# A two-layer trunk on one core: layer B's projection weights are split earlier and pass DRAM

## The chip, the core and the metric

The kernel runs on one core of a Trainium2 chip. The engines of the core are TensorE (PE), VectorE (DVE), ScalarE (ACT), GpSimd (POOL) and SyncE (SP), which issues most transfers. The metric is the device time in microseconds, the median of several runs. The kernel before takes 1478.44 us (three runs, 1476.97 to 1478.71).

## The reference

A sequence of 1024 rows of width 1024 passes two layers, both with an adaptive norm in front and a gated residual behind. Layer A is a gated delta rule over 8 heads of width 128. After it a shared pair of keys and values is computed once; layer B attends to it with 16 heads of width 64 and "stick-breaking" weights in place of a softmax:

```python
kv = hk @ w_kv                                      # keys and values, once
proj = h @ w_in_b                                   # layer B: queries and a gate
q = rms(proj[..., :W]);  z = proj[..., W:]
logits = q @ k.T * Dh ** -0.5
after = sum(log_keep) - cumsum(log_keep)            # log_keep = log_sigmoid(-logits), masked
o = exp(log_sigmoid(logits) + after) @ v
y = (o * silu(z)) @ w_out
```

All inputs and the output are 32-bit floats. `w_in_b` is 1024 x 2048: 1024 columns of queries, 1024 of the gate.

## The kernel before

Every product that needs full precision is done in three matmuls over operands that are split into a high and a low part: high is the operand rounded to the matmul's own 32-bit format, low is what is left (`mm3`, L110 to L113: high x high, high x low, low x high). A weight tile is loaded into `wraw` (`load_w`, L198 to L201), copied on ACT into `whi` (L194) and subtracted on DVE into `wlo` (L195). The pool `wp` holds two buffers of each.

The kernel has these stages, in order: layer A's projections and delta rule; layer A's out projection; the shared keys and values, which take up from about 690 us; layer B; and the final out projection.

Keys and values (`keys_values`, L837 to L853): eight column groups `n` of `w_kv`, 256 columns each. The first four are keys, the last four are values (the values' half). For every `n` there are two halves of the rows, and in each four steps; a step is 24 matmuls of 256 columns into one of two PSUM banks (`pj`), which ACT evacuates to `kv` (L797). Keys get a norm and are transposed; values are only stored to `v_dram` (L808, L809). After each `n`, `mod_b` prepares one eighth of layer B's input `hT`: ACT modulates it, DVE casts the high part (L834), POOL subtracts the low part (L835).

Layer B works on 8 pairs of heads. A pair has a query projection (`stage_q`, L942) and a gate projection (`stage_z`, L957). Each begins by loading and splitting one weight tile of 1024 x 128, 512 KB, so there are 16 such tiles; in order of use they are q0, z0, q1, z1 and so on. One projection is two halves of the rows with 24 matmuls of 512 columns each. Behind a half of the queries ACT makes `sqq` and the two `Qs` (L951 to L953) and DVE their low parts (L954, L955); behind a half of the gate there is `szb` (L963, L964). The attention of a pair runs between: logits on PE (L976, L977), a sigmoid on ACT (L978, `kp`), a scan on DVE (L982), transposes on PE (L997, `ptw`), the split of the weights into `wh` on ACT (L1002) and `wl` on DVE (L1004), the product with the values on PE (L1022, L1023, `pa`), and its collection in `o` (L1032, L1033).

What sets the order: PE's order is written by hand from a list of positions in time, so that steps of a projection lie between attention steps of another pair (L1098 to L1151). The order on ACT, DVE, POOL and in the DMA queues is laid by a scheduler when the kernel is built; on the chip every engine then works strictly in that order. SP issues one transfer after the other, and one that has to wait for a buffer holds those behind it.

Of the kernel before, what the change touches and what calls it, by code (L numbers as in the profile page):

```python
# [8 lines left out]
F32 = mybir.dt.float32  # L9
F32R = mybir.dt.float32r  # L10
I32 = mybir.dt.int32
AF = mybir.ActivationFunctionType
ALU = mybir.AluOpType
# [9 lines left out]
def kernel(  # L23
# [24 lines left out]
    V, S, G, PE = nc.vector, nc.scalar, nc.gpsimd, nc.tensor  # L48
    dma = nc.sync.dma_start

    P = 128
    T = x.shape[1]
    D = x.shape[2]
    NT = T // P
    ND = D // P
    HA = 8
    NC = T // P
    NPB = 8
# [8 lines left out]
    wp = ctx.enter_context(tc.tile_pool(name="wp", bufs=2, side="left"))  # L67
    dr = ctx.enter_context(tc.tile_pool(name="dr", bufs=1, space=DRAM))
# [54 lines left out]
    kTd = dr.tile([2, NPB, P, T], F32, name="kT_dram")  # L123

    vd = dr.tile([NPB, P + 1, NT, 2 * HD], F32, name="v_dram")
    gTd = dr.tile([HA * NC, P], F32, name="gT_dram")
    gate_d = dr.tile([2, D], F32, name="gate_dram")

# [61 lines left out]
    def split_w(raw, shape, pool=None, eng=None, copy=None):  # L190

        hi = (pool or wp).tile(shape, F32R, name="whi", tag="whi")
        lo = (pool or wp).tile(shape, F32R, name="wlo", tag="wlo")
        (copy or S.copy)(out=hi, in_=raw)  # L194
        (eng or G).tensor_tensor(out=lo, in0=raw, in1=hi, op=ALU.subtract)  # L195
        return hi, lo

    def load_w(src):  # L198
        raw = wp.tile([P, src.shape[0] // P, src.shape[1]], F32, name="wraw", tag="wraw")
        dma(out=raw, in_=src.rearrange("(k p) n -> p k n", p=P))  # L200
        return raw  # L201
# [151 lines left out]
    with tc.tile_pool(name="gt", bufs=1, side="right", reuse_waits="tile") as gt:  # L353
        hi, lo = w_first[0]
# [5 lines left out]
        for cc in range(NC):  # L360
# [8 lines left out]
                        op=ALU.add)  # L369
# [287 lines left out]
    for h in range(HA):  # L657
# [23 lines left out]
        if h < len(mods):  # L681
            i, part = mods[h]
# [35 lines left out]
    kp_ = kv_stack.enter_context(tc.tile_pool(name="kvp", bufs=2, side="right", reuse_waits="tile"))  # L718

    def x4(shape, dtype, name):  # L720
        return kp_.tile(shape, dtype, name=name, tag="x4", bufs=8)
# [50 lines left out]
    def kv_weights(n):  # L772
        c0 = n * 256
        parts = []
        for k0 in (0, 4):
            raw = load_w(w_kv[k0 * P:(k0 + 4) * P, c0:c0 + 256])
            if k0 == 0:
                parts.append(split_w(raw, [P, 4, 256], None, V))
            else:
                hi, lo = x4([P, 4, 256], F32R, "kwh"), x4([P, 4, 256], F32R, "kwl")  # L780
                S.copy(out=hi, in_=raw)
                V.tensor_tensor(out=lo, in0=raw, in1=hi, op=ALU.subtract)
                parts.append((hi, lo))
        return parts
# [42 lines left out]
    def mod_b(n):  # L827

        xh = x4([P, T], F32, "xhl")
        dma(out=xh, in_=xhT[n])  # L830
        S.activation(out=xh, in_=xh, func=AF.Identity, scale=mod_gs[1][:, n:n + 1], bias=mod_sh[1][:, n:n + 1])
        for hf in range(TH):
            xs = xh[:, hf * 512:hf * 512 + 512]
            V.tensor_copy(out=hT[hf][:, 0, n], in_=xs)  # L834
            G.tensor_tensor(out=hT[hf][:, 1, n], in0=xs, in1=hT[hf][:, 0, n], op=ALU.subtract)  # L835

    def keys_values():  # L837
        parts, tail = kv_weights(0), None
        yield
        for n in range(8):  # L840
            for hf in range(TH):
                if hf == 1 and n < 7:
                    nxt = kv_weights(n + 1)
                g = kv_half(n, parts, hf)
                for i in range(4):
                    next(g)
                    if i == 2 and tail:
                        next(tail, None)
                    yield
                tail = g  # L850
            parts = nxt
            mod_b(n)
        next(tail, None)  # L853

    with tc.manual_schedule(engines={PE.engine}):
        ra, kv = [rest_of_a(t) for t in range(NT)], keys_values()
        for step in "01203w142k53k64k75kk6k7k":
            next(kv if step in "wk" else ra[int(step)], None)
        for _ in kv:
            pass  # L860
# [54 lines left out]
    def project_steps(hi, lo, hf):  # L915
        ps = pj_pool.tile([P, 512], F32, name="pj", tag="pj")
        for k in range(ND):
            mm3(ps, hi[:, k], lo[:, k], hT[hf][:, 0, k], hT[hf][:, 1, k], k == 0, k == ND - 1)
            if k == 5 and sqs:
                norms(*next(iter(sqs)))  # L920
            if k < ND - 1:
                yield
        return ps
# [3 lines left out]
    def norms(p, hf):  # L927
# [7 lines left out]
        if hf == 0:  # L935
# [3 lines left out]
        V.tensor_scalar(out=nrq[p].rearrange("p t e -> p (t e)"), in0=rn, scalar1=-HD ** -0.5, scalar2=None,  # L939
                        op0=ALU.mult)  # L940

    def stage_q(p):  # L942

        q0, q1 = Qs[p, 0], Qs[p, 1] = [bp.tile([P, T], F32R, name="Qs", tag="Qs", bufs=4) for _ in range(2)]
        hi, lo = split_w(load_w(w_in_b[0][:, p * P:(p + 1) * P]), [P, ND, P], None, V)
        n2[p] = bp.tile([P, 16], F32, name="n2q", tag="n2q", bufs=2)
        for hf in range(TH):
            ps = yield from project_steps(hi, lo, hf)
            ts_ = slice(hf * 512, hf * 512 + 512)
            sqs[p, hf] = sq = bp.tile([P, 512], F32, name="sqq", tag="sqq", bufs=1)  # L950
            S.activation(out=sq, in_=ps, func=AF.Square)  # L951
            S.copy(out=q0[lo_, ts_], in_=ps[lo_])
            S.copy(out=q1[up_, ts_], in_=ps[up_])  # L953
            V.tensor_tensor(out=q0[up_, ts_], in0=ps[lo_], in1=q0[lo_, ts_], op=ALU.subtract)  # L954
            V.tensor_tensor(out=q1[lo_, ts_], in0=ps[up_], in1=q1[up_, ts_], op=ALU.subtract)  # L955
            yield
    def stage_z(p):  # L957

        hi, lo = split_w(load_w(w_in_b[0][:, D + p * P:D + (p + 1) * P]), [P, ND, P], None, V)
        for hf in (1, 0):  # L960
            ps = yield from project_steps(hi, lo, hf)
            sz[p, hf] = s = bp.tile([P, 512], F32, name="szb", tag="szb", bufs=3)
            S.activation(out=s, in_=ps, func=AF.Sigmoid)  # L963
            V.tensor_tensor(out=s, in0=ps, in1=s, op=ALU.mult)  # L964
            yield

    def weigh(p, e, t):

        n = (t + 1) * P
        d = slice(t * P, (t + 1) * P)  # L970
        q, kh, kl = Qs[p, e], Kh[p, e], Kl[p, e]
        kps[p, e, t] = kp = bp.tile([P, T], F32, name="kp", tag="kp", bufs=KPB)
        for s0 in range(0, n, 512):
            sw = min(512, n - s0)
            pl = lg_pool.tile([P, 512], F32, name="pl", tag="lg")
            PE.matmul(pl[:, :sw], q[:, d], kh[:, s0:s0 + sw], start=True, stop=False)  # L976
            PE.matmul(pl[:, :sw], q[:, d], kl[:, s0:s0 + sw], start=False, stop=True)  # L977
            S.activation(out=kp[:, s0:s0 + sw], in_=pl[:, :sw], func=AF.Sigmoid, scale=nrq[p][:, t, e:e + 1])  # L978
            if s0 + sw < n:
                yield  # L980
        kr = kp[:, :n][:, ::-1]
        V.tensor_tensor_scan(out=kr, data0=kr, data1=stick[:, T - n:][:, ::-1], initial=1.0, op0=ALU.mult,  # L982
                             op1=ALU.max)
        weighed.add((p, e, t))
        yield
# [54 lines left out]
    def projections():  # L1040
        for p in range(NPB):
            if p > 0:
                yield from stage_z(p - 1)
            yield from stage_q(p)
        yield from stage_z(NPB - 1)
# [78 lines left out]
    for i, (p, e, t) in enumerate(tiles):  # L1124
        w = weigh(p, e, t)
# [10 lines left out]
    n = 32 * NPB - 22  # L1136
# [45 lines left out]
```

## Time and profile before

| | |
|---|---|
| median of three runs | 1478.44 us |
| the profiled execution | 1474.96 us |
| its span | 1473.2 us |
| PE busy | 1378.9 us (94% of the span) |
| DVE busy | 1047.4 us (71%) |
| ACT busy | 743.7 us (50%) |
| POOL busy | 105.5 us (7%) |
| DMA | 181.15 MB, mean 123 GB/s |

One execution was profiled, and its rows are in microseconds from the start of the span. A row of the profile names a line of the kernel (L111), an engine, an operation and the tiles that it writes and reads (`out<-in`). "Idle" is the time that an engine sat without work before an instruction, with what released it. The matmuls of PE are pipelined, so their durations overlap: one of 512 columns adds about 0.23 us to the chain though it is shown with 0.4.

### The profile page before, as it was taken

The page shows a single profiled execution, that of the slowest core. Times are in us where ns is not written, and L with a number is a line of the kernel's source. Part 1 is how long each engine was busy: PE and PEld are TensorE (multiplying, and loading weights), DVE is VectorE, ACT ScalarE, POOL GpSimd, SP SyncE. Part 2 cuts the span into 40 slices and gives each one's busy share as a digit, 9 for nine tenths or more (in the row PEclk, how much of TensorE's full clock was granted, in tenths as well). Part 3 has the DMA queues.
Part 4 walks back from the last instruction along what each step waited for, and adds up shares of the span by engine and source line. Part 5 has one row for each costly group of instructions (what it writes and reads, how often), then busy time and mean ns, then how long its engine had stood idle before and what let it go on. Part 6 is the DMA issues. An engine that isn't in the chain of part 4 may idle for free.

```text
span 1473.2 us, 23359 instructions
## 1 busy us (share of the span) xinstructions
PE 1378.9 (94%) x8611; PEld 1151.5 (78%) x8611; DVE 1047.4 (71%) x2465; ACT 743.7 (50%) x1494; POOL 105.5 (7%) x105
## 2 busy tenths in 40 slices
PE   3789999999979999999799999999999999998998
PEld 0468888787867887878589999878888888885676
DVE  3768796969778787954786611388888888889332
ACT  5366645555554655431774522366666666665110
POOL 1300000000000000000220101311011011000000
PEclk9999999999989999999999999999999999999999
DMA  9244214454444353454854443624234233233511
GB/s 327 63 120 141 70 50 115 116 142 105 129 108 140 90 165 102 134 156 150 288 180 158 144 144 101 194 72 107 59 93 115 69 99 92 68 97 124 178 56 58
DMA packets 168132, 181.15 MB, mean 123 GB/s; under 512 B 36617, under 2 KB 121426, under 8 KB 168018
## 3 DMA queue, kind: packets, MB, share of 16 engines
q1 hardware_dynamic: 165586, 171.27, 38.9%
q0 software_dynamic: 2432, 8.39, 1.6%
q8 instruction: 68, 1.11, 0.3%
q14 instruction: 46, 0.38, 0.1%
HBM read 140.22 MB, written 39.40 MB: 122 GB/s over the span
## 4 chain that ended last, share of the span: by engine, by line
PE 62%; DVE 24%; ACT 6%; DMA 4%; issue 3%; SPq 0%; POOL 0%; DVEq 0%; ACTq 0%; POOLq 0%
PE pj L111 15%; PE pj L113 15%; PE pj L112 14%; DVE kp L982 8%; DVE wl L1004 2%; PE pgr L484 2%; PE ptw L997 2%; DMA mraw<-in_w_ada_dram 2%; DVE macc L150 2%; PE pa L1022 1%; PE pa L1023 1%; PE pc L174 1%; PE pl L976 1%; ACT kp L978 1%; PE pl L977 1%
## 5 line engine op out<-in xcount | busy, mean ns | idle before, releaser
L111 PE MATMUL pj<-hT,whi 128*128 128x512 f32 (+1 forms) x528 | 215.3, 408 | 6.4 <-ACT vT L421 3.5
L113 PE MATMUL pj<-hT,wlo 128*128 128x512 f32 (+1 forms) x528 | 214.5, 407 | 4.6 <-DVE wlo L195 4.4
L112 PE MATMUL pj<-hT,whi 128*128 128x512 f32 (+1 forms) x528 | 214.3, 406 | 1.3 <-POOL hT L309 1.3
L982 DVE TENSOR_TENSOR_SCAN kp<-kp,stick 128x896 f32<-128x896 f32 (+7 forms) x128 | 179.4, 1403 | 2.4 <-ACT kp L978 1.5
L978 ACT ACTIVATE kp<-pl,nrq 128x512 f32<-128x512 f32 (+1 forms) x192 | 107.0, 581 | 44.8 <-PE pl L977 36.6
L1002 ACT ACTIVATE wh<-ptw 128x512 fp32r<-128x512 f32 (+3 forms) x152 | 84.6, 557 | 74.3 <-PE ptw L997 72.6
L111 PEld LDWEIGHTS pj<-hT,whi 128*128 128x128 f32 (+1 forms) x528 | 98.4, 186 | 25.5 <-ACT vT L421 4.2
L113 PEld LDWEIGHTS pj<-hT,wlo 128*128 128x128 f32 (+1 forms) x528 | 98.4, 187 | 23.4 <-DVE wlo L195 5.8
L112 PEld LDWEIGHTS pj<-hT,whi 128*128 128x128 f32 (+1 forms) x528 | 98.3, 186 | 19.7 <-POOL hT L309 2.3
L111 PE MATMUL pj<-hbT,whi 128*128 128x512 f32 x256 | 107.4, 419 | 0.0
L195 DVE TENSOR_TENSOR wlo<-wraw,whi 128x1024 fp32r<-128x1024 f32 x55 | 67.3, 1223 | 56.3 <-ACT whi L194 49.8
L111 PE MATMUL pj<-wo,oh 128*128 128x512 f32 x256 | 103.5, 406 | 3.9 <-ACT oh L237 2.3
L113 PE MATMUL pj<-wo,ol 128*128 128x512 f32 x256 | 101.5, 397 | 0.5 <-DVE ol L238 0.5
L112 PE MATMUL pj<-wo,oh 128*128 128x512 f32 x256 | 101.8, 398 | 0.0
L113 PE MATMUL pj<-hbT,wlo 128*128 128x512 f32 x256 | 100.8, 394 | 0.0
L112 PE MATMUL pj<-hbT,whi 128*128 128x512 f32 x256 | 100.1, 391 | 0.0
L997 PE MATMUL ptw<-ident,kp 128*128 128x128 f32 x576 | 91.0, 276 | 8.1 <-DVE wl L1004 6.0
L1004 DVE SCALAR_TENSOR_TENSOR wl<-ptw,wh 128x512 fp32r<-128x512 f32 (+1 forms) x140 | 87.4, 625 | 10.3 <-ACT wh L1002 9.2
L194 ACT CAST whi<-wraw 128x1024 fp32r<-128x1024 f32 x55 | 57.8, 1051 | 67.9 <-PE pj L112 60.4
L1022 PE MATMUL pa<-wh,vt 128*128 128x256 f32 (+1 forms) x280 | 79.2, 305 | 13.0 <-DVE o L1033 11.8
L997 PEld LDWEIGHTS ptw<-ident,kp 128*128 128x128 f32 x576 | 67.8, 141 | 27.0 <-DVE wl L1004 12.7
L150 DVE SCALAR_TENSOR_TENSOR macc<-mraw,cact,macc 128x512 f32<-128x512 f32 x105 | 82.4, 785 | 5.4 <-DMA mraw<-in_w_ada_dram 4.2
(303 smaller groups left out, 3391.5 us busy)
## 6 DMA issues: line engine op xcount, KB each, us to landing
mraw<-in_w_ada_dram SPq DMA_DIRECT2D x96, 256.0 KB
wraw<-in_w_in_a_dram SPq DMA_DIRECT2D x32, 512.0 KB
mraw<-in_w_ada_kv_dram SPq DMA_DIRECT2D x32, 256.0 KB
xr<-x_dram SPq DMA_DIRECT2D x16, 512.0 KB
wraw<-in_w_kv_dram SPq DMA_DIRECT2D x16, 512.0 KB
kT_dram<-kt SPq DMA_DIRECT2D x32, 256.0 KB
wraw<-in_w_in_b_dram SPq DMA_DIRECT2D x16, 512.0 KB
Kh<-kT_dram SPq DMA_DIRECT2D x32, 256.0 KB
```

The costliest lines, as they stand in the source:

```text
L111: PE.matmul(ps, lh, rh, start=start, stop=False)
L112: PE.matmul(ps, lh, rl, start=False, stop=False)
L113: PE.matmul(ps, ll, rh, start=False, stop=stop)
L150: V.scalar_tensor_tensor(out=acc, in0=raw, scalar=cact[:, k:k + 1], in1=acc, op0=ALU.mult, op1=ALU.add)
L194: (copy or S.copy)(out=hi, in_=raw)
L195: (eng or G).tensor_tensor(out=lo, in0=raw, in1=hi, op=ALU.subtract)
L978: S.activation(out=kp[:, s0:s0 + sw], in_=pl[:, :sw], func=AF.Sigmoid, scale=nrq[p][:, t, e:e + 1])
L982: V.tensor_tensor_scan(out=kr, data0=kr, data1=stick[:, T - n:][:, ::-1], initial=1.0, op0=ALU.mult, op1=ALU.max)
L997: PE.transpose(pt[:, i], kps[p, e, 2 * g + q][:, j * P:(j + 1) * P], ident)
L1002: S.activation(out=wh[:, :nb], in_=pt[:, :nb], func=AF.Copy, bias=-1.0)
L1004: V.scalar_tensor_tensor(out=wl[:, :nb], in0=pt[:, :nb], scalar=-1.0, in1=wh[:, :nb], op0=ALU.add, op1=ALU.subtract)
L1022: PE.matmul(dst, lh, wh[:, sl], start=(j == 0), stop=False)
```

## The change

Fifteen of the sixteen weight tiles of layer B (all but q0) are split ahead of time. `presplit` is a generator of 30 steps, one for each half (512 rows) of a tile. A step loads 256 KB of raw weights on SP's queue, copies the high part on ACT, subtracts the low part in place on DVE, and stores both, 256 KB each, to the new DRAM tensor `wb_dram` from POOL's queue. Its tiles share the tag `x2k`, five buffers of 2 KB a partition, which the keys used. One step is taken after each of the 32 steps of the values' half. In layer B `weights_b` then loads the two parts, 512 KB each, straight into the buffers `whi` and `wlo`; for q0 it loads and splits as before.

```diff
+    wbd = dr.tile([2 * NPB, P, 2, ND * P], F32, name="wb_dram")
...
+    def column_of(i):
+        return i // 2 * P + (D if i % 2 else 0)
+    def presplit():
+        for i in range(1, 2 * NPB):
+            for kh in range(2):
+                src = w_in_b[0][kh * 512:kh * 512 + 512, column_of(i):column_of(i) + P]
+                raw = kp_.tile([P, 4, P], F32, name="wbr", tag="x2k", bufs=5)
+                dma(out=raw, in_=src.rearrange("(k p) n -> p k n", p=P))
+                hi = kp_.tile([P, 4, P], F32R, name="wbh", tag="x2k", bufs=5)
+                S.copy(out=hi, in_=raw)
+                lo = raw.bitcast(F32R)
+                V.tensor_tensor(out=lo, in0=raw, in1=hi, op=ALU.subtract)
+                for j, w in enumerate((hi, lo)):
+                    G.dma_start(out=wbd[i, :, j, kh * 512:kh * 512 + 512],
+                                in_=w.bitcast(F32).rearrange("p k n -> p (k n)"))
+                yield
     def keys_values():
+        pre = presplit()
...
                     if i == 2 and tail:
                         next(tail, None)
+                    if n >= 4:
+                        next(pre, None)
                     yield
...
+    def weights_b(i):
+        if i == 0:
+            return split_w(load_w(w_in_b[0][:, 0:P]), [P, ND, P], None, V)
+        parts = wp.tile([P, ND, P], F32R, name="whi", tag="whi"), wp.tile([P, ND, P], F32R, name="wlo", tag="wlo")
+        for j in range(2):
+            dma(out=parts[j].bitcast(F32).rearrange("p k n -> p (k n)"), in_=wbd[i, :, j])
+        return parts
     def stage_q(p):
-        hi, lo = split_w(load_w(w_in_b[0][:, p * P:(p + 1) * P]), [P, ND, P], None, V)
+        hi, lo = weights_b(2 * p)
...
     def stage_z(p):
-        hi, lo = split_w(load_w(w_in_b[0][:, D + p * P:D + (p + 1) * P]), [P, ND, P], None, V)
+        hi, lo = weights_b(2 * p + 1)
```

## Rows read from the trace of the kernel before

**Rows 1.** Busy time by stretch (engine us, instructions), TensorE's clock, DMA share, GB/s.

```profile
core 0: us, PE busy (x) PEld busy (x) DVE busy (x) ACT busy (x) POOL busy (x), PEclk, DMA share, GB/s
10.00:20.00 10.00, 0.00 (x0) 0.00 (x0) 3.94 (x15) 6.79 (x9) 0.00 (x0) 1.00 1.03 403
711.00:720.00 9.00, 4.58 (x24) 3.34 (x22) 6.75 (x16) 6.95 (x16) 2.66 (x4) 1.00 0.96 325
842.00:933.00 91.00, 91.00 (x770) 91.00 (x769) 15.60 (x25) 24.88 (x45) 10.64 (x10) 1.00 0.38 118
933.00:950.00 17.00, 16.98 (x84) 14.02 (x82) 5.18 (x7) 5.88 (x10) 4.67 (x7) 1.00 0.92 247
1000.00:1300.00 300.00, 288.94 (x1764) 248.31 (x1762) 261.17 (x391) 191.46 (x362) 29.81 (x21) 1.00 0.33 91
```

**Rows 2.** Waits of PE, 950 to 1310: us in total, times, longest us.

```profile
PE pa L1022 <- DVE o L1033: 6.8, 9, 1.1
PE ptw L997 <- DVE wl L1004: 5.3, 7, 1.0
```

**Rows 3.** The chain of waits around 1040: start us, us, what.

```profile
1039.18 0.24 PE pj L112
...
1039.45 1.05 ACT whi L194
1040.50 0.49 ACT sqq L951
...
1045.72 0.32 DVE o L1033
```

**Rows 4.** PE's timeline at three holes, idle before in brackets: start us, us, instruction.

```profile
992.74 0.39 PE L1022 MATMUL pa<-wh,vt 128*128 128x256 f32 x1 [1.06 <-DVE o L1033]
...
1046.10 0.39 PE L1022 MATMUL pa<-wh,vt 128*128 128x256 f32 x1 [1.05 <-DVE o L1033]
...
1258.73 0.39 PE L1022 MATMUL pa<-wh,vt 128*128 128x256 f32 x1 [1.06 <-DVE o L1033]
```

**Rows 5.** Lines of the splits: count, ns min/median/max, first and last start.

```profile
L194 ACT CAST whi<-wraw x55: 1033/1049/1120, 73.7 to 1278.7; 128x1024 fp32r<-128x1024 f32 x55
L195 DVE TENSOR_TENSOR wlo<-wraw,whi x55: 1196/1224/1260, 74.8 to 1279.8; 128x1024 fp32r<-128x1024 f32 x55
L822 ACT CAST kt<-pk x16: 567/587/653, 765.2 to 850.6; 128x512 fp32r<-128x512 f32 x16
L823 DVE TENSOR_TENSOR kt<-pk,kt x16: 679/681/692, 766.1 to 851.3; 128x512 fp32r<-128x512 f32 x16
```

**Rows 6.** Timelines of DVE and PE where layer B starts.

```profile
962.48 1.20 DVE L195 TENSOR_TENSOR wlo<-wraw,whi 128x1024 fp32r<-128x1024 f32 x1
...
966.31 0.55 PE L997 MATMUL ptw<-ident,kp 128*128 128x128 f32 x3 [0.78 <-DVE wl L1004]
```

**Rows 7.** Groups by line, 842 to 933: busy us, mean ns, idle before.

```profile
L797 ACT COPY kv<-pj 128x256 f32<-128x256 f32 x31 | 11.6, 373 | 59.3 <-PE pj L113 56.7 <-DMA v_dram<-kv 2.5
```

**Rows 8.** DMA queues, 1041.5 to 1048, one raw load: packets, MB, share.

```profile
q1 hardware_dynamic: 1040, 0.52, 27.7%
```

**Rows 9.** DMA queues, 850.6 to 853.7, stores of `kt`.

```profile
q1 hardware_dynamic: 454, 0.82, 70.6%
```

**Rows 10.** DMA queues, 740 to 745, stores of POOL's queue.

```profile
q0 software_dynamic: 303, 1.05, 63.0%
```

**Rows 11.** POOL's stores of `xh`, 256 KB each: issue in ns.

```profile
L752 POOL DMA_DIRECT2D xhT_dram<-xh x16: 750/752/1071, 709.0 to 761.9; - x16
```

**Rows 12.** POOL's timeline before layer B, 925 to 960.

```profile
930.29 2.65 POOL L835 TENSOR_TENSOR hbT<-xhl,hbT 128x512 fp32r<-128x512 f32 x2 [20.86 <-DVE hbT L834]
```

**Rows 13.** SP's timeline at the entry and in the steady part.

```profile
935.13 1.46 SPq L896 DMA_DIRECT2D Kh<-kT_dram  x2
...
1041.79 0.39 SPq L200 DMA_DIRECT2D wraw<-in_w_in_b_dram  x1
1051.26 1.17 SPq L896 DMA_DIRECT2D Kh<-kT_dram  x2
```

## The prediction

> **What bounds the kernel now.** I read the table of stretches first. It splits the part that the change touches into three: the values' half of the keys and values stage (842 to 933 us), the entry into layer B (933 to 950) and the steady part of layer B (1000 to 1300). In the values' half PE is busy for all of its 91.00 us, while DVE works 15.60 and ACT 24.88 of them and the DMA engines 0.38 [rows 1]. So PE sets the length there, and the spare time on ACT, DVE and DMA is what the change wants to use. In layer B PE is busy 288.94 of 300 us and DVE 261.17: PE again, with small holes. The waits of PE name them: between 950 and 1310 us it lost 6.8 us in 9 waits for `o` and 5.3 in 7 waits for `wl` [rows 2]. One more wait of 0.6 us, for the first nrq, is left out. About 12 us is thus the most that relief of ACT and DVE can give back in layer B, and only where a split stands in front of the hole.
>
> The chain of waits then says where that is. Every 53 us it runs PE, then the copy to `whi` (1.05 us on ACT), then `sqq` and `Qs`, then DVE, and ends in `o`, for which PE waits [rows 3]. That hole of PE is 1.06 us at 992.74, 1.05 at 1046.10 and 1.06 at 1258.73; it comes six times, once for each pair of heads [rows 4].
>
> **The change part by part.**
>
> Removed from layer B: 15 of its 16 splits, each one copy on ACT (1.049 us) and one subtraction on DVE (1.224 us) [rows 5], so 15.7 us of ACT and 18.4 us of DVE. Half of them, those at the end of a gate projection, stand where PE is dense, with no wait of PE behind them, and give nothing. The others sit between the end of the query projection and its evacuation. There the copy starts at 1039.45 because PE has just read the buffer for the last time (L112 ends at 1039.42), and one more matmul of 0.24 us, L113, ends the projection at 1039.66; but `sqq` stands behind the copy and starts at 1040.50 [rows 3]. Without the copy it can start 0.84 us earlier. DVE's subtraction falls into the same stretch and goes too, so nothing else on DVE holds the evacuation. The chain down to `o` shifts by that 0.84, and the hole of 1.05 shrinks to 0.2. Six times 0.84 is 5.0 us. Bounds: nothing, if DVE's backlog of scans takes the place of the copy, and 6 x 1.06 = 6.4 if the whole hole closes. A seventh place is at the start: DVE's subtraction at 962.48 lies in a row of scans and ends just before PE's hole of 0.78 us at 966.31 [rows 6]. 1.2 us less on DVE closes it: 0.8 us. What is late next is the other hole in a pair, in which PE waits for `wl` behind two scans after the first half of the queries; no split stands there and I leave it. Gain in layer B: 5.8 us.
>
> Added to the values' half: 30 steps, each with a copy of 128x512 on ACT and a subtraction of 128x512 on DVE. The same shapes take 0.587 and 0.681 us in the keys [rows 5]. They sum to 17.6 us on ACT and 20.4 on DVE, beside 24.88 and 15.60 that are busy of 91 [rows 1]; PE's work covers them. If the cover goes, because a copy stands in ACT's order and its data has not come, the evacuation behind it (L797) is late and PE has one other PSUM bank. ACT now idles 59.3 us before the 31 evacuations of this stretch, 1.9 us each [rows 7]; a delay below that is free.
>
> Added to the DMA queues: per step a raw load of 256 KB on SP's queue in runs of 512 bytes, and two stores of 256 KB on POOL's. A 512 KB load of that kind took 27.7% of 6.5 us on all 16 engines, 1.80 us, so 0.90 for half of it [rows 8]. For a store there are two neighbours: 0.82 MB of `kt` stores in 70.6% of 3.1 us [rows 9], which is 374 GB/s or 1.40 us for the two, and 1.05 MB of POOL's stores in 63.0% of 5 us [rows 10], which is 333 GB/s or 1.57. A step is 2.30 to 2.47 us, 30 steps 69 to 74. The stretch already holds 0.38 x 91 = 34.6 us of transfers, so the demand is 104 to 109 us in a time of 91: 13 to 18 too much. From the other side, 10.7 MB (118 GB/s over 91 us) and 23.6 MB at the 403 GB/s of 10 to 20 us [rows 1] take 85 us and fit. What doesn't fit need not reach PE: no matmul before 944 reads these tensors, and only five 2 KB buffers feed the transfers, so the queues ahead of the kernel's own transfers stay short. I take no cost here and keep 0 to 18.
>
> POOL issues 60 stores at 0.752 us [rows 11], 45 us beside its 10.64 [rows 1]; it fits. But the low half of `hT` (L835) stands in the same order and ends at 931.7 and 932.9, some 5 us before PE needs the last of it (the 22nd matmul of 0.23 us after 933) [rows 12]: POOL must not sit on a store whose data is late for longer than that.
>
> Layer B's loads: the weights come as 1 MB instead of 0.5, straight into `whi` and `wlo`, so the load waits on SP until PE has left the buffer, where a split waited on ACT. In the steady part SP issues such a load at 1041.79 and nothing until the K loads at 1051.26 [rows 13], so nothing is kept waiting behind it, and 2.8 us of transfer at 374 GB/s have the other projection's 26 us (half the distance of two holes) as cover. Cost nothing; without the cover, 2.8 us for each of 15. At the entry it is tighter: 933 to 950 is already 0.92 busy with K and V [rows 1], which leaves 1.4 us, and the first presplit tile brings 2.8 us of transfers, where before the raw tile was already in SBUF. SP must place it ahead of the K loads at 935.13 [rows 13]. 2.8 - 1.4 = 1.4 us is my cost; 0 and 2.8 are its bounds, and more if unfinished presplit stores are in the way.
>
> Sum on the profiled execution (1474.96 us, the span of 1473.2 and 1.8 around it): 1474.96 - 5.8 + 1.4 = 1470.6. The median of the three timed runs lies 3.5 us above that execution, so the prediction is 1474.0.
>
> **A rule against it.** The 403 GB/s of 10 to 20 us is the best rate that the table shows, over loads alone [rows 1]. The Trainium skill, DMA: Bandwidth & Descriptors, Specifications, gives a core about 358 GB/s from HBM. By that figure the 34.3 MB of the values' half would take an estimated 95.9 us, 4.9 more than there are; by the row they take 85 and fit. The row disagrees with the figure, and rival (d) below, which comes out likewise, has a small chance.
>
> **The rivals.**
>
> (a) DMA becomes the bound of the values' half. Between 711 and 720, where both queues ran together, the engines were 0.96 busy at 325 GB/s [rows 1]; 34.3 MB at that rate are 105.5 us. The raw loads wait on SP for buffers that POOL's stores still read, V's stores stand behind them, and the copies on ACT hold the evacuations. It decides once the presplit lags by more than the 1.9 us of ACT's idle time. Price 14.5 us less some 3 of slack, and the gain of 5.8 stays: 1478.4 + 11.5 - 4.4 = 1485.5, slower. For it: 0.38 and 69 us of transfers exceed the stretch. Against: nothing in the stretch depends on the presplit's end.
>
> (b) The gain doesn't come. DVE is busy 87% of the steady part; if the scans move up and the hole stays, only the 0.8 us and the entry's 1.4 count: 1479.0, no change.
>
> (c) The relief is worth more: the order on ACT and DVE is fixed at build and is laid anew with 34 us less work, and the waits of rows 2 close altogether: 12.1 us, 1466.3 to 1468.
>
> (d) DMA binds, but mildly: at 364 GB/s, the mean of the two busy rows (325 and 403) [rows 1], the 34.3 MB take 94.2 us. PE is held 3.2 us in the values' half against 4.4 gained: 1477.2, no change. For and against as in (a).
>
> **How the numbers follow.** Chances: the forecast 0.40, (a) 0.28, (b) 0.17, (c) 0.10, (d) 0.05. The forecast's own range is 1471 to 1477. Taking in (a) up to 1489 and (c) down to 1467 leaves out less than 2 in 10. A measurement here tells 0.2%, 3 us, from no change, so faster is below 1475.5 and slower above 1481.4. Faster: three quarters of the forecast, (c) and a little of (a) and (b): 0.44. Slower: most of (a), some of (b) and (d): 0.30. Same: 0.26.
>
> **What would show it.** Right: in the values' half PE stays at 1.00 of its time with the DMA share above 0.9, the 1.05 us holes after the second half of the queries shrink to 0.2, and the stretch from 1000 to 1300 is 5 us shorter. Wrong in (a): L797 waits for DMA or PE's share falls below 0.95 before 933, and the values' half grows by 5 us or more. Wrong at the entry: PE waits for `whi` or `wlo` from DMA near 945 or 960. Wrong in layer B: the same holes with DVE as releaser and no `whi` copy before them.

## The result and the profile after

The changed kernel takes 1502.58 us (median of 5 runs, 1500.22 to 1506.87), the kernel before 1478.44 (5 runs, 1476.30 to 1481.37). The ratio is 1.0167, with a 95% interval of 1.0153 to 1.0181: 24 us slower, where 4.4 us faster was forecast. The profiled executions span 1501.8 and 1473.2 us.

The table of stretches of the kernel after shows where. Its columns are the stretch, its length, the busy time of PE, PE's weight loads, DVE, ACT and POOL with instruction counts, PE's granted clock, the DMA share and GB/s:

```profile
842.00:933.00 91.00, 77.83 (x615) 76.60 (x614) 33.62 (x46) 33.93 (x63) 30.95 (x48) 0.94 0.88 283
845.10:962.65 117.55, 100.36 (x776) 98.51 (x774) 39.19 (x54) 40.01 (x76) 39.55 (x63) 0.93 0.88 284
933.00:950.00 17.00, 16.55 (x128) 16.34 (x127) 4.58 (x6) 4.40 (x10) 6.32 (x11) 0.91 0.83 259
1000.00:1300.00 300.00, 293.97 (x1804) 254.84 (x1803) 252.32 (x393) 185.93 (x358) 29.59 (x23) 1.00 0.39 114
```

In [rows 1] PE filled 842 to 933 completely, at a clock of 1.00 and a DMA share of 0.38. Now it works 77.83 of these 91 us. The second line is the whole values' half, from the evacuation of the last keys to that of the last values: 117.5 us, against 92.0 before (841.1 to 933.1), with the same matmuls. Of the 25.5 us more, PE is idle for 17.2 (117.55 less 100.36). The other 8.4 are busy time (100.36 against 92.00), which the clock of 0.93 goes with. In the last line layer B is fuller than before: 293.97 us of PE busy in 300, against 288.94 [rows 1].

What PE, ACT and POOL waited for between 840 and 1020 us in the kernel after (engine and line, releaser: us in total, times, longest), and below it the same for SP's queue from 845 to 1010:

```profile
ACT wbh L851 <- DMA wbr<-in_w_in_b_dram: 57.8, 25, 5.8
POOL vraw L935 <- DMA vraw<-v_dram: 29.9, 2, 15.6
PE pj L111 <- ACT kv L799: 17.3, 9, 4.9
ACT vt L937 <- POOL vraw L935: 9.8, 2, 9.2
PE pl L1010 <- ACT kp L1012: 5.5, 1, 5.5
```

```profile
SPq L849 <- DMA wb_dram<-wbr: 54.1, 17, 7.0
```

PE waits for evacuations (L799, L797 before), nine times. ACT waits for the raw loads of the early split, and SP, which issues these loads, waits for POOL's stores to land, since they hold the buffers. The chain of waits puts the three in one line (start, duration, what; "SPq" and "POOLq" are queues), ahead of the longest pause of PE:

```profile
920.54 0.54 POOL wb_dram L855
921.08 0.17 issue
921.25 0.01 POOLq L855
921.26 4.86 DMA wb_dram<-wbr
926.13 0.02 SPq L849
926.15 0.03 issue
926.18 4.58 DMA wbr<-in_w_in_b_dram
930.76 0.02 issue
930.78 0.04 ACTq L851
930.82 0.04 issue
930.86 0.63 ACT wbh L851
```

The timeline of ACT and the one of PE show what stands behind that copy (start, duration, instruction; in brackets the idle time before it and its releaser):

```profile
923.14 0.37 ACT L799 COPY kv<-pj 128x256 f32<-128x256 f32 x1
928.15 0.62 ACT L851 CAST wbh<-wbr 128x512 fp32r<-128x512 f32 x1 [4.64 <-DMA wbr<-in_w_in_b_dram]
929.41 1.24 ACT L833 ACTIVATE xhl<-xhl,sh,gs 128x1024 f32<-128x1024 f32 x1 [0.65 <-DMA xhl<-xhT_dram]
930.86 0.62 ACT L851 CAST wbh<-wbr 128x512 fp32r<-128x512 f32 x1 [0.20 <-DMA wbr<-in_w_in_b_dram]
931.38 0.36 ACT L799 COPY kv<-pj 128x256 f32<-128x256 f32 x1
```

```profile
926.59 0.28 PE L113 MATMUL pj<-kwh,hkT 128*128 128x256 f32 x1
931.80 0.58 PE L111 MATMUL pj<-whi,hkT 128*128 128x256 f32 x1 [4.93 <-ACT kv L799]
932.18 0.41 PE L112 MATMUL pj<-wlo,hkT 128*128 128x256 f32 x1
932.39 0.41 PE L113 MATMUL pj<-whi,hkT 128*128 128x256 f32 x1
```

A store takes 4.86 us to land, the load that needs its buffer 4.58 more, and the copy (L851) stands on ACT ahead of the evacuation at 931.38. In the kernel before, evacuations come 2.85 us apart where PE runs through; this one came 8.2 us after the one at 923.14, and PE sat idle 4.93 us. The table of stretches again, for two stretches behind a pause (the first behind one of 2.23 us) and, between them, one in full swing:

```profile
870.50:875.00 4.50, 4.06 (x21) 4.06 (x22) 2.87 (x3) 1.62 (x5) 3.69 (x4) 0.62 0.74 240
912.00:916.00 4.00, 4.00 (x36) 4.00 (x35) 0.69 (x1) 0.89 (x2) 1.08 (x2) 1.00 1.02 380
931.80:936.00 4.20, 4.20 (x19) 4.20 (x20) 3.71 (x3) 1.78 (x3) 3.74 (x5) 0.50 0.85 271
```

In the last the granted clock is 0.50 for 4.2 us, the lower level (1.2 GHz), and 19 matmuls run where 36 ran in 4.0 us at 1.00. At the full level a matmul comes every 0.119 us; 19 take 19 x 0.119 = 2.3 us, so the pause costs an estimated 1.9 us more than it lasts.

In layer B, PE's waits for `o` and `wl` between 950 and 1310 us are down from 12.1 us [rows 2] to 5.3, and the hole of 1.05 [rows 4] is 0.35:

```profile
PE pa L1056 <- DVE o L1067: 2.7, 10, 0.4
PE ptw L1031 <- DVE wl L1038: 2.6, 6, 0.6
```

```profile
1027.62 0.39 PE L1056 MATMUL pa<-wh,vt 128*128 128x256 f32 x1 [0.34 <-DVE o L1067]
1287.29 0.38 PE L1056 MATMUL pa<-wh,vt 128*128 128x256 f32 x1 [0.35 <-DVE o L1067]
```

These are the first and the sixth hole of that kind, five pairs of heads apart: a pair takes 51.9 us in the mean ((1287.29 - 1027.62) / 5) where it took 53.2 ((1258.73 - 992.74) / 5, rows 4). The account of the spans, 28.6 us: 4.0 lie before the values' half, where the number of instructions on each engine is the same in both kernels, so these are taken as how one execution differs from another; 25.5 in the values' half; 5.3 at the entry, up to the first hole (1027.62 against 992.74; PE waits 5.5 us for `kp`, which stands on ACT behind a `vt` whose V load came late); minus 6.3 in the five pairs; the rest is rounding.

### The profile page after: what moved, and what is told of

The parts are those of the page before. It is cut to its first block, busy times and chain, and to the rows that moved or that the text cites. A ratio compares the mean times of both kernels' runs of the same rounds, so it can differ in the third digit from the quotient of the medians.

```text
span 1501.8 us, 23658 instructions
## 1 busy us (share of the span) xinstructions
PE 1391.7 (93%) x8611; PEld 1164.0 (78%) x8611; DVE 1052.4 (70%) x2480; ACT 747.7 (50%) x1509; POOL 131.8 (9%) x165
## 4 chain that ended last, share of the span: by engine, by line
PE 54%; DVE 24%; DMA 8%; ACT 6%; issue 5%; POOL 1%; SPq 1%; DVEq 0%; ACTq 0%; POOLq 0%
PE pj L111 13%; PE pj L113 12%; PE pj L112 12%; DVE kp L1016 7%; DVE wl L1038 2%; DMA mraw<-in_w_ada_dram 2%; PE pgr L486 2%; PE ptw L1031 2%; DVE macc L152 2%; PE pa L1056 1%; PE pa L1057 1%; DMA wb_dram<-wbr 1%; PE pc L176 1%; PE pl L1010 1%; POOL wb_dram L855 1%
## 5 line engine op out<-in xcount | busy, mean ns | idle before, releaser
L1016 DVE TENSOR_TENSOR_SCAN kp<-kp,stick 128x896 f32<-128x896 f32 (+7 forms) x128 | 175.8, 1374 | 7.8 <-ACT kp L1012 6.1
L111 PE MATMUL pj<-whi,hkT 128*128 128x256 f32 x256 | 76.6, 299 | 18.5 <-ACT kv L799 16.0
L113 PE MATMUL pj<-whi,hkT 128*128 128x256 f32 x256 | 74.6, 292 | 0.2 <-DVE hkT L760 0.2
```

The lines of the kernel that those rows point to most:

```text
L111: PE.matmul(ps, lh, rh, start=start, stop=False)
L113: PE.matmul(ps, ll, rh, start=False, stop=stop)
```

## The experiments

Theory A: the early split itself costs the loss, nearly all of it in the values' half, and the relief of layer B is real. Three carriers were possible for that loss: the copy's place in ACT's order (A1 in the expectations), the transfers themselves (A2, by way of V's stores), and SP's queue, in which a load waits for stores (A3). The rival: layer B's new loads cost, not the early split. The table sums up the values' half, from the last keys' to the last values' evacuation, in each kernel's profile; PE idle is the length less PE's busy time.

| kernel | values' half | PE idle | clock | DMA share | GB/s |
|---|---|---|---|---|---|
| before | 92.0 | 0.0 | 1.00 | 0.38 | 120 |
| after | 117.5 | 17.2 | 0.93 | 0.88 | 284 |
| early split alone | 117.8 | 16.3 | 0.93 | 0.89 | 284 |
| layer B alone | 92.0 | 0.0 | 1.00 | 0.44 | 138 |
| copy on DVE | 116.3 | 19.3 | 0.93 | 0.88 | 284 |
| raw loads on POOL, copy on DVE | 111.1 | 13.4 | 0.94 | 0.86 | 279 |
| queries' tiles only | 100.7 | 5.9 | 0.98 | 0.70 | 220 |
| thin stores | 101.9 | 6.6 | 0.98 | 0.73 | 221 |
| seven buffers | 115.3 | 16.4 | 0.96 | 0.90 | 291 |

The lines of the early split alone and of the thin stores, on which most hangs, in the columns of the table of stretches:

```profile
844.30:962.10 117.80, 101.52 (x779) 99.54 (x778) 41.57 (x54) 40.93 (x76) 39.91 (x64) 0.93 0.89 284
844.10:946.00 101.90, 95.32 (x779) 94.21 (x778) 42.12 (x54) 40.50 (x76) 39.46 (x63) 0.98 0.73 221
```

**The early split alone.** Layer B loads and splits every tile as before.

```diff
-        if i == 0:
-            return split_w(load_w(w_in_b[0][:, 0:P]), [P, ND, P], None, V)
+        if True:
+            return split_w(load_w(w_in_b[0][:, column_of(i):column_of(i) + P]), [P, ND, P], None, V)
```

> All 30 steps of the early split stay in the values' half, but layer B loads and splits its 16 tiles as before and doesn't read the new DRAM tensor. Theory A (the early split itself costs: its raw loads wait on SP for buffers that POOL's stores still read, the copy on ACT waits for the load, the evacuation stands behind the copy): the values' half takes 115 to 120 us as in the changed kernel, against 92.0 before, and the time is 1500 to 1512, above the changed kernel, since layer B's gain is missing. Theory B (the loss is in layer B's own loads, 1 MB a tile in place of 0.5, and at its entry): the values' half takes below 100 us and the time is below 1485.

Measured: 1509.84 us, ratio 1.0214 (1.0195 to 1.0233). The whole loss is there, and without layer B's change it is 7 us larger. Of it 25.8 us lie in the values' half; at the entry PE waits 4.9 us for `kp`. Theory A holds.

**Layer B alone.** Only z0 is split early, and all tiles from z0 on are loaded from its place, so layer B computes with one tile's weights.

```diff
-        for i in range(1, 2 * NPB):
+        for i in range(1, 2):
...
-            dma(out=parts[j].bitcast(F32).rearrange("p k n -> p (k n)"), in_=wbd[i, :, j])
+            dma(out=parts[j].bitcast(F32).rearrange("p k n -> p (k n)"), in_=wbd[1, :, j])
```

> Only tile z0 is split early (2 steps in place of 30), and all tiles from z0 on are loaded from that one place, so layer B's loads, queues and engines are as in the changed kernel but its weights are wrong. Theory A: the values' half is back at 92 to 94 us with the clock at 1.00, layer B keeps its period of 51.8 us a pair (53.2 before), and the time is 1467 to 1472. Theory B: the entry still loses 5 us or more and the time is above 1478.

Measured: 1472.29 us, ratio 0.9962 (0.9949 to 0.9975), some 6 us faster. The values' half is 92.0 us again, the pairs take 52.0 in the mean and their hole is 0.35. So the gain forecast for layer B is there, near its forecast size, and the 1 MB loads don't eat it. The entry has one wait of 3.6 us for `kp` and loses 3.0 us up to the first hole, without the early split's 28 other steps. The rival falls as the cause of the 25 us; it keeps at most these 3.

**The copy on DVE.**

```diff
-                S.copy(out=hi, in_=raw)
+                V.tensor_copy(out=hi, in_=raw)
```

> The changed kernel with the copies of the early split on DVE in place of ACT; bytes, buffers and queues are the same. If ACT's order carries the lag to PE (A1): PE waits below 5 us in the values' half, which takes 92 to 100 us, the split runs on into layer B, and the time is 1475 to 1488. If the transfers carry it themselves, through V's stores on SP's queue behind the blocked raw loads and the kv buffers (A2): PE still waits over 10 us, now with V's stores as the cause, and the time stays above 1493.

Measured: 1502.99 us, ratio 1.0163 (1.0140 to 1.0187), as the changed kernel. The waits of the values' half show what took the copy's place:

```profile
DVE wbh L851 <- DMA wbr<-in_w_in_b_dram: 54.7, 22, 4.7
ACT xhl L833 <- DMA xhl<-xhT_dram: 34.4, 4, 13.6
PE pj L111 <- ACT kv L799: 17.5, 3, 9.8
```

No copy of the early split stands ahead of the evacuations now, but one of the kernel's own loads (`xhl`, L833) comes up to 13.6 us late, and the evacuations wait behind it. ACT only carries the delay; A1 falls. A2's number came, but not by V's stores, as it had it.

**The raw loads on POOL's queue, the copy on DVE.**

```diff
-                dma(out=raw, in_=src.rearrange("(k p) n -> p k n", p=P))
+                G.dma_start(out=raw, in_=src.rearrange("(k p) n -> p k n", p=P))
...
-                S.copy(out=hi, in_=raw)
+                V.tensor_copy(out=hi, in_=raw)
```

> The changed kernel with the raw loads of the early split on POOL's queue in place of SP's and the copies on DVE; bytes and buffers are the same. Theory A3 (SP's order carries the lag: a raw load that waits for a buffer holds the loads of xhl and the stores of V behind it, and ACT then waits for xhl): PE waits below 5 us in the values' half, which takes 92 to 96 us with the clock at 1.00; the rest of the early split runs beside layer B's entry; time 1474 to 1486. Rival (the DMA engines are simply full, so xhl and V's stores are late on any queue): PE waits over 10 us again and the time is above 1493.

Measured: 1508.89 us, ratio 1.0194 (1.0172 to 1.0216). Nothing of the early split stands on SP or ACT any more, and `xhl` still comes late, with DMA engines 0.86 busy. The values' half is 6 us shorter, but PE waits 9.4 us behind it for the part of `hT` that the late `xhl` feeds. The wait of ACT for `xhl`, and what SP waits for:

```profile
ACT xhl L833 <- DMA xhl<-xhT_dram: 28.6, 4, 9.2
SPq L202 <- DVE wlo L197: 16.2, 2, 12.2
SPq L1120 <- DVE wlo L197: 11.5, 1, 11.5
SPq L202 <- DVE kwl L784: 7.3, 1, 7.3
```

So the early split's loads on SP aren't the cause, and A3 falls in that form. SP is not out of it, though: it waits 35 us for DVE's subtractions of the kernel's own weights, which now stand behind the early split's copies on DVE. The second `xhl` is issued at 891.23, 2.4 us after ACT is free for it, and ACT starts on it 6.8 us later still. From issue to ACT's start the four take 5.7 to 8.2 us, where the kernel before took 3.4 to 4.2. A late issue and a slower transfer share the wait, and no run separates them.

**The queries' tiles only**: 14 of the 30 steps, the gate's tiles split in layer B as before.

```diff
-        for i in range(1, 2 * NPB):
+        for i in range(2, 2 * NPB, 2):
...
-                    if n >= 4:
+                    if n >= 4 and i % 2:
...
-        if i == 0:
-            return split_w(load_w(w_in_b[0][:, 0:P]), [P, ND, P], None, V)
+        if i == 0 or i % 2:
+            return split_w(load_w(w_in_b[0][:, column_of(i):column_of(i) + P]), [P, ND, P], None, V)
```

> Only the seven query tiles q1 to q7 are split early, 14 steps, one behind every second step of the values' half; gate tiles are split in layer B as before. Theory A with the hole of PE closed by the query tiles' splits alone: 33 us of added transfers and 35 of old ones fit into 92 us, PE doesn't wait in the values' half, the period of a pair is near 52 us, and the time is 1468 to 1474. Rival (any raw load with so few buffers stalls ACT, or the gates' splits bring half of the gain): the values' half grows by 4 us or more, or the period stays above 52.8, and the time is 1476 or more.

Measured: 1483.31 us, ratio 1.0037 (1.0024 to 1.0049). The forecast of theory A missed and the rival's came: less than half of the steps still costs 8.7 us in the values' half. The steps don't spread over the stretch (the last of the 14 copies starts at 911.9), and the table of stretches of this kernel shows what that does:

```profile
860.00:920.00 60.00, 54.13 (x435) 53.10 (x434) 18.18 (x21) 18.61 (x37) 19.88 (x30) 0.97 0.84 264
920.00:944.55 24.55, 24.55 (x208) 24.54 (x207) 3.66 (x6) 7.43 (x14) 6.32 (x5) 1.00 0.29 88
```

PE loses its 5.9 us in the first stretch, at a DMA share of 0.84, and nothing in the second, at 0.29. A mean share of 0.70 hides that.

**Thin stores**: the early split alone (layer B as before), each store writing a quarter of its columns.

```diff
-                    G.dma_start(out=wbd[i, :, j, kh * 512:kh * 512 + 512],
-                                in_=w.bitcast(F32).rearrange("p k n -> p (k n)"))
+                    G.dma_start(out=wbd[i, :, j, kh * 512:kh * 512 + 128],
+                                in_=w.bitcast(F32).rearrange("p k n -> p (k n)")[:, 0:128])
```

> The early split alone (as the first experiment, 1509.8 us), but each of the 60 stores writes only the first quarter of its columns: 64 KB in place of 256; layer B splits its own tiles. Same instructions, same queues, 11.8 MB of stores less. If the bytes make the stores late and so the buffers and the raw loads (bandwidth): the values' half is back at 92 to 97 us and the time at 1478 to 1486. If the fixed time from issue to landing does, with five buffers: the values' half stays above 108 us and the time above 1495.

Measured: 1492.14 us, ratio 1.0086 (1.0057 to 1.0115), against 1509.84 for the same kernel with whole stores. Every instruction, load and wait of the early split is there, only 11.8 MB of stores are gone (60 x 256 KB x 0.75), and the values' half falls from 117.8 to 101.9 us. So 16 of the 26 us go with the stored bytes. The result lies between the two forecasts (92 to 97 us for bytes, above 108 for the fixed time of a store): the other 10 us stay although the DMA engines are 0.73 busy. A store of 64 KB still takes a median of 3.3 to 3.4 us to land, SP still waits 45.7 us for stores, and ACT 39.7 us for the raw loads, in 22 waits of at most 3.7.

**Seven buffers** for the early split's tiles, where there were five (and one less for `x4`, to make room).

```diff
-                raw = kp_.tile([P, 4, P], F32, name="wbr", tag="x2k", bufs=5)
+                raw = kp_.tile([P, 4, P], F32, name="wbr", tag="x2k", bufs=7)
...
-        return kp_.tile(shape, dtype, name=name, tag="x4", bufs=8)
+        return kp_.tile(shape, dtype, name=name, tag="x4", bufs=7)
```

> The changed kernel with seven buffers of the tag x2k in place of five, and seven of x4 in place of eight. If the number of buffers limits the early split (raw loads wait for stores to land): the wait of SP for those stores falls from 54 us to below 25 and the values' half from 117.5 us to 105 or less, time below 1492. If the transfers' bytes limit it, the values' half stays within 3 us of 117.5 and the time above 1498.

Measured: 1504.04 us, ratio 1.0166 (1.0136 to 1.0197). The waits of ACT and PE, and of SP's queue, in the values' half:

```profile
ACT wbh L851 <- DMA wbr<-in_w_in_b_dram: 48.4, 18, 5.9
PE pj L111 <- ACT kv L799: 13.0, 7, 5.1
SPq L849 <- DMA wb_dram<-wbr: 15.8, 6, 4.0
```

SP waits 15.8 us for stores instead of 54.1, but ACT still waits 48.4 us for the loads (57.8 in the table above), and the values' half is only 2 us shorter. The stores land later: a median of 5.6 us for the low parts, against 4.6 with five buffers. With whole stores the number of buffers was thus not what limits; more transfers in flight took longer each, on engines that are 0.88 to 0.90 busy.

**Pauses of PE without the early split.** To see whether the lower clock goes with PE's pauses or with the early split's work on the other engines, ACT was slowed in the kernel before, three times with a different edit: 13 evacuations at 8 places, 24 at 4 places, and 19 copies of the bank onto itself at 4 places.

```diff
-            S.copy(out=kv[:, t], in_=ps[:, :256])
+            for _ in range(13 if n >= 4 and t == 1 else 1):
+                S.copy(out=kv[:, t], in_=ps[:, :256])
```

> What the lower granted clock of the values' half is from. The kernel before, with no early split and no added transfer; in the values' half the evacuation of one group in four (8 places) is done 13 times over (13 x 0.372 = 4.8 us on ACT instead of 0.37), so that PE waits some 2 us for its bank, 8 times, 15 to 18 us in all, as it waited 17.3 us in the changed kernel. If PE's pauses are what the clock falls after, the granted clock of the stretch falls below 0.97 and the stretch grows by clearly more than the waits: some 20 to 26 us for 15 to 18 of waits, and the time is 1498 to 1504. If the clock fell for the early split's own work (ACT, DVE, POOL and DMA engines busy at once), it stays at 1.00, the stretch grows by the waits alone, and the time is 1493 to 1497.

> As the kernel with 13 evacuations at 8 places, in which PE paused 11 times by at most 0.9 us, 7.4 us in all, and its clock stayed at 1.00; now fewer and longer pauses: the kernel before without early split or added transfers, 4 evacuations of the values' half done 24 times over (24 x 0.372 = 8.9 us of ACT), so that PE pauses some 4 to 5 us four times, 16 to 20 us in all, as the longest pause of the changed kernel (4.93 us, after which a matmul came every 0.213 us instead of 0.119 for 4.1 us). If the clock falls after long pauses of PE, whatever the other engines do, it shows 0.50 for some 4 us behind each, the stretch loses some 1.8 us more per pause (7 in all, and grows by 23 to 28 us), and the time is 1500 to 1507. If the fall came from the early split's work on the other engines, the clock stays at 1.00, the stretch grows by the pauses and modelled ends alone, 17 to 21, and the time is 1494 to 1499.

> The run with 24 evacuations at 4 places paused PE by 1.0 us at most, so it said nothing on long pauses (its clock stayed at 1.00). Here, in the kernel before and without early split or added transfers, 4 tiles of the values' half are copied onto themselves in PSUM 19 times ahead of their evacuation (19 x 0.37 to 0.45 = 7 to 8.5 us of ACT), so that the bank itself is held: PE runs one tile on (2.85 us) and pauses 4.5 to 6 us, four times, 18 to 24 in all. If the clock falls after long pauses of PE whatever the other engines do, it shows 0.50 for some 4 us behind each pause, the stretch from the last keys to the last values grows by the pauses and 6 to 9 us more, and the time is 1501 to 1510. If the fall came from the early split's work on the other engines, the clock stays at 1.00, the stretch grows by the pauses alone, and the time is 1495 to 1502.

Measured: 1489.46 us (ratio 1.0074, 1.0047 to 1.0101), 1484.74 (1.0045, 1.0029 to 1.0060) and 1484.28 (1.0056, 1.0034 to 1.0077). All three missed what they were made for. The waits of PE in the three kernels, in this order:

```profile
PE pj L111 <- ACT kv L798: 7.4, 11, 0.9
```

```profile
PE pj L111 <- ACT kv L798: 5.2, 7, 1.0
```

```profile
PE pj L111 <- ACT kv L799: 4.7, 7, 1.0
```

No pause is longer than 1.0 us, and the clock is 1.00 in all three. The order on ACT is laid at build, and there the added copies are known: other evacuations were placed between them. A late transfer isn't known at build, and nothing is moved around it. What follows is one half only: 7 to 11 pauses of up to 1.0 us don't lower the clock. The other half can be read in two traces without the transfers of an early split around the pause, the first two lines in the kernel before, in layer A, the third at the entry of layer B alone, behind its wait of 3.6 us:

```profile
413.52 4.27 PE L484 MATMUL pgr<-qk 128*128 128x256 f32 x8 [2.69 <-ACT kdec L457]
414.00:416.00 2.00, 1.88 (x5) 0.98 (x5) 2.00 (x6) 1.97 (x6) 0.00 (x0) 0.50 0.00 0
962.00:966.00 4.00, 4.00 (x9) 3.13 (x10) 3.48 (x2) 1.68 (x3) 1.67 (x2) 0.50 0.13 53
```

The granted clock is 0.50 in both, at a DMA share of 0.00 and 0.13. So it falls behind a pause without the early split and its transfers. That the pause alone does it isn't isolated: ACT and DVE were at work in both places, and a pause of 2.31 us before 704.28 in the kernel before left the clock at 1.00.

**A split on POOL instead**, in the kernel before, without early split: from q2 and z1 on, POOL does both the copy and the subtraction in layer B.

```diff
-        hi, lo = split_w(load_w(w_in_b[0][:, p * P:(p + 1) * P]), [P, ND, P], None, V)
+        hi, lo = split_w(load_w(w_in_b[0][:, p * P:(p + 1) * P]), [P, ND, P], None, *((G, G.tensor_copy) if p > 1 else (V,)))
...
-        hi, lo = split_w(load_w(w_in_b[0][:, D + p * P:D + (p + 1) * P]), [P, ND, P], None, V)
+        hi, lo = split_w(load_w(w_in_b[0][:, D + p * P:D + (p + 1) * P]), [P, ND, P], None, *((G, G.tensor_copy) if p > 0 else (V,)))
```

> The kernel before, with no early split: the tiles from q2 and z1 on are still split in layer B, but both the copy and the subtraction stand on POOL, which is busy 30 of 300 us there. If the gain comes from taking the copy away in front of the queries' evacuation on ACT (and the subtraction from DVE): the period of a pair is about 51.8 us as in the changed kernel, PE's hole of 1.05 us shrinks to 0.35, no byte is added, and the time is 1470 to 1474. If POOL's slower split or its order behind the values' preparation makes the weights late, PE waits for wlo and the time is 1478 or more.

Measured: 1476.07 us, ratio 0.9973 (0.9961 to 0.9986): some 3 to 4 us faster than the kernel before and 26 than the changed one. It lies between the two forecasts (1470 to 1474, 1478 or more). The groups of POOL's instructions in layer B (1000 to 1300; count, busy us, mean ns, idle before and its releaser) show what it costs there:

```profile
L195 POOL TENSOR_TENSOR wlo<-wraw,whi 128x1024 fp32r<-128x1024 f32 x11 | 32.7, 2976 | 0.9
L194 POOL CAST whi<-wraw 128x1024 fp32r<-128x1024 f32 x11 | 11.5, 1044 | 145.8 <-PE pj L112 145.8
```

4.0 us a tile, on an engine that is busy 30 of the 300 us in the kernel before [rows 1]. ACT and DVE get most of the relief that the early split was to buy (the hole at `o` is 0.41, a pair takes 52.2 us), and no byte is added to DRAM's traffic. At the entry PE waits once, 2.0 us, for `wl`, where it waited 0.8 [rows 6].

## Why the prediction was wrong

**The step that failed** is the one on the DMA queues in the values' half: "What doesn't fit need not reach PE", and from it "I take no cost here and keep 0 to 18". It measured 25.5 us, past its own upper bound.

The demand in front of that sentence was right. It came to 104 to 109 us of DMA time in a stretch of 91; in the trace the engines were busy 0.88 of 117.55 us, 103.4. Set aside was what follows from it. The argument was that no matmul before 944 reads these tensors and that five buffers keep the queues short. But the early split shares its engines' orders with the kernel's own work: the copy stands on ACT ahead of an evacuation, and where it doesn't (copy on DVE), a late `xhl` does. PE depends on the next instruction in ACT's order, not on the end of the early split. That a delay below 1.9 us is free [rows 7] is not refuted; the evacuation ahead of the longest pause was 5.4 us late (8.2 less 2.85).

**The two ends of the range were badly chosen.** The low end, 85 us, was made with the 403 GB/s of [rows 1], a stretch of plain loads. The values' half is a mixture (raw loads in runs of 512 bytes, stores from POOL's queue, V's stores), and it ran at 284 GB/s at a share of 0.88, or an estimated 323 if it were full. The row of the same kind was there: 325 GB/s at 0.96, between 711 and 720 [rows 1]. The Trainium skill, DMA: Bandwidth & Descriptors, Specifications, whose 358 GB/s the prediction set aside for the row of 403, was nearer than that row, and still too high for this mixture. The high end, 18 us, was demand less time. It left out that the engines don't fill all of the time (14.1 us of the stretch, 117.5 less 103.4), and that PE's clock falls behind long pauses (8.4 us more of busy time, of which an estimated 1.4 at most are the modelled ends of the matmuls before nine pauses). These two are the same loss seen from two sides and don't add up. Why the engines don't fill is not shown: with seven buffers SP's waits for stores are down to 15.8 us, and the share is still 0.90.

**Rival (a)** had the mechanism, the place and the sign: SP's loads wait for stores, copies on ACT hold the evacuations, L797 is late. Its price of 11.5 us was less than half of what came. Only a part of its story was tested away: the buffers it names are not what limits (seven buffers).

**Layer B's gain** was forecast at 5.8 us. Alone, the median falls by some 6 us (0.9962), and in its profiled execution the five pairs gain 6.2 us and the entry loses 3.0. In the pairs of the changed kernel the hole went from 1.05 to 0.35 where 0.2 was forecast. The pair's other hole, which was left at nothing, shrank too (`wl`: 5.3 us in 7 waits to 2.6 in 6), and a pair gains 1.3 us in the mean and not 0.84. Size about right, division wrong. Rival (b) falls; (c) had half of its 12.1 us, since 6.8 came.

**The entry** was costed at 1.4 us, bounds 0 to 2.8, as a wait for the first early tile. It cost 5.3, and not there: PE never waited for `whi` or `wlo` from DMA by more than 0.5 us, but for `kp` behind a late V load, 5.5 us. The clock is 0.50 behind that wait. That wait is 3.6 us with layer B alone and 4.9 with the early split alone, so neither part accounts for it by itself.

**POOL and the arithmetic.** 0.54 us for a store where 0.75 was taken, 0.62 for a copy (0.587) and 0.69 for a subtraction (0.681) are near enough; they were never what counted.

**What stays open.** Ten of the 26 us remain when three quarters of the stored bytes are gone. Whether they go with the raw loads' bytes or with the time that a small store takes to land wasn't separated; thin stores with seven buffers would be the next kernel. That the clock falls for PE's long pauses, and for nothing else, isn't shown either.

## What to carry to other kernels

Work that is moved "under" a stage with idle engines must fit the stage's transfers as well: add up the DMA time by the row of the same mixture, and if it exceeds the stretch, forecast the excess as the least cost. A demand that fits isn't free for that: the thin stores lost 10 us at a share of 0.73. Don't ask whether the bound engine reads the moved data, but which instruction stands behind the moved one on each engine that serves it; a late transfer holds everything in that order. And look for an idle engine at the place itself, here POOL in layer B, before sending data through DRAM.

## What the runs showed of the hardware

The granted clock of the values' half was 1.00 in the kernel before. In the changed one it fell to 0.50 for some 4 us behind the longest pause (4.93 us), and from 870.5 to 875.0, behind a pause of 2.23, it was 0.62 in the mean; four pauses of 0.45 to 0.80 in the same trace and 25 of at most 1.0 in the three slowed kernels left it at 1.00. In the kernel before, with no early split, it was 0.50 behind a pause of 2.69 us at a DMA share of 0.00. A store of 256 KB from POOL's queue landed in a median of 4.5 and 4.6 us here (high and low parts), one of 64 KB in 3.3 to 3.4. The same DMA engines moved 323 GB/s between 880 and 900 us, at a share of 0.97, and 403 under plain loads [rows 1]: the busy share and the rate are two things, and only the row of the same mixture gives both.
